# 10,564 products of constants ahead of a decoder step's first conditioning product

## The chip, the cores and the metric

The kernel runs on one core of a Trainium2 chip. The metric is device time in microseconds of one execution; lower is better. A core has a matrix engine (TensorE, PE in the profile, with PEld for its loads of the stationary operand), VectorE (DVE), ScalarE (ACT), GpSimd (POOL) and SyncE (SP, which here only issues DMAs).

## What is computed

One step of a one-layer decoder with D = 2048: T = 288 tokens (256 of a prompt and 8 x 4 samples), all in float32. Cut to what matters here:

```
mod = silu(c) @ w_ada + b_ada                  # 9 conditioning vectors, 2048 x 12288
h = rms(x, g_mix) * (1 + sc_m) + sh_m
proj = h @ w_in                                # 2048 x 9216, then split
ya = b_gate * conv(c_gate * hc)                # short causal convolution
yb = gelu(u) * spatial(rms(gelu(v), g_v))      # 128 x 128 mixing in each chunk
merged = sigmoid(ga) * (ya @ w_pa) + sigmoid(gb) * (yb @ w_pb)
x = x + gt_m * (merged @ w_out)
h2 = rms(x, g_ffn) * (1 + sc_f) + sh_f
gate, up = split(h2 @ w_ffn_in)
x = x + gt_f * ((silu(gate) * up) @ w_ffn_out)
y = rms(x, g_final)
```

## The kernel before

Activations stand transposed, features on the 128 partitions and the 288 tokens along the row. Each weight matrix comes from HBM as blocks of up to 128 x 2048 float32 in tiles tagged `raw`; there are seven such buffers, and a new tile takes the one that comes free first. A block is split by ScalarE and VectorE into a high part `hi` in float32r and a remainder `lo` in float32r (`split`, L448 and L454). A float32 product is made of three float32r products, high by high, high by low and low by high, added in PSUM (`triple`, L224, L227 and L229, or L226 where the order is turned). Nearly all of TensorE's work is this. `ada` products (L388) are the conditioning, plain float32 on 32-column strips of the array.

TensorE's order is the program's order. At the head ScalarE, VectorE and SyncE are put in program order too, up to the point where the early jobs are done; what is recorded ahead of the head is placed by a scheduler. The head is this, in order of TensorE: 24 bf16 products of constant ones into a PSUM tile `idle` that nobody reads (`warm`, L571), the conditioning blocks `a0` with a few more such products between, the first tile of x scaled (`first_tile`), the weights `w0`, the conditioning blocks `a1` (two blocks, the first run after the eighth column tile of `w0`), then `wK`, `wA` and so on:

```
    def warm(n, out=None):
        out = idle if out is None else out
        for _ in range(n):
            PE.matmul(out[:, :T], wb[:, :P], wb, start=True, stop=True)
    ...
    steps = [Do(lambda: warm(24)), a0[0], Do(lambda: warm(5)), a0[1]]
    steps += [Do(first_tile), Do(lambda: warm(6))]
```

SyncE issues the loads in one queue: a0 (two buffers), w0, x's first tile, a1 (two), x's second tile, wK, wA, more of x and wA; in the head each of the seven buffers is taken once before one is taken again. On ScalarE the first compute is `ctt` (half of silu of c), on VectorE the constants `ones`, `mhalf`, `cs`, and then the second half of `ctt` and `cs` (L156, L157).

Of the kernel before, what the change touches and what calls it, by code (L numbers as in the profile page):

```python
# [8 lines left out]
F32 = mybir.dt.float32  # L9
F32R = mybir.dt.float32r  # L10
# [4 lines left out]
P = 128  # L15
D = 2048
T = 288
# [7 lines left out]
RAW = 7  # L25
# [59 lines left out]
def decoder_kernel(tc, d):  # L85
    nc = tc.nc
    from contextlib import ExitStack

    with ExitStack() as es:
        def pool(name, bufs=1, **kw):  # L90
            return es.enter_context(tc.tile_pool(name=name, bufs=bufs, **kw))

        pc = pool("const")
        pw = pool("wstream")
        pslot = pool("slots", SLOTS)
        ptmp = pool("tmp", 5)
        pps = pool("psum", 4, space=bass.MemoryType.PSUM)
        with tc.manual_schedule(engines={nc.tensor.engine}):
            _body(tc, nc, d, pc, pw, pslot, ptmp, pps)


def _body(tc, nc, d, pc, pw, pslot, ptmp, pps):
    ids = [0]

    def nm(s):
        ids[0] += 1
        return f"{s}_{ids[0]}"

    def const(name, shape, dt=F32):
        return pc.tile(shape, dt, tag=name, name=name)  # L110
# [7 lines left out]
    def psmain():  # L118
        return pps.tile([P, 512], F32, tag="main", name=nm("pm"), bufs=4)
# [4 lines left out]
    V, A, G, PE, SY = nc.vector, nc.scalar, nc.gpsimd, nc.tensor, nc.sync  # L124
# [227 lines left out]
    class Step:  # L352
        defer = False
        raw = None
# [209 lines left out]
    wb = const("wb", [P, 288], BF16)  # L564
    G.memset(wb, 1.0)
    idle = psmain()
# [475 lines left out]
        tail.close()  # L1042


    rh1 = h1.__getitem__
    def at(main, plan):
        out, n = [], 0
        for s in main:
            out.append(s)
            if isinstance(s, Blk):  # L1050
                n += 1
                out += plan.pop(n, [])
        assert not plan
        return out
# [101 lines left out]
    for s in steps:  # L1156
# [11 lines left out]
        i = pos[id(s)]  # L1168
# [124 lines left out]
```

## Time and profile before

| | |
|---|---|
| median of 2 runs | 1625.62 us (1625.25 to 1626.0) |
| the profiled execution | 1625.02 us, its span 1623.2 us |
| TensorE busy | 1613.2 us, 99% of the span, 12,645 products |
| VectorE, ScalarE busy | 1015.8 us (63%), 736.2 us (45%) |
| mean granted TensorE clock | 0.998 |
| HBM read | 352.46 MB |

Busy time counts overlapping products once in the engine's total; a group's own busy time adds up the durations of its instructions, which overlap. The digits in the page's strips are tenths of a slice of a fortieth of the span. In a row of the view by windows stand the window, its length, the busy time (and count) of PE, PEld, DVE, ACT and POOL, the granted clock, the DMA share and GB/s. In the timeline stand start, duration, engine (SPq is SyncE's queue), line, operation, and in brackets the idle time ahead and what ended it.

### The profile page before, as it was taken

The page shows a single profiled execution, that of the slowest core. Times are in us where ns is not written, and L with a number is a line of the kernel's source. Part 1 is how long each engine was busy: PE and PEld are TensorE (multiplying, and loading weights), DVE is VectorE, ACT ScalarE, POOL GpSimd, SP SyncE. Part 2 cuts the span into 40 slices and gives each one's busy share as a digit, 9 for nine tenths or more (in the row PEclk, how much of TensorE's full clock was granted, in tenths as well). Part 3 has the DMA queues.
Part 4 walks back from the last instruction along what each step waited for, and adds up shares of the span by engine and source line. Part 5 has one row for each costly group of instructions (what it writes and reads, how often), then busy time and mean ns, then how long its engine had stood idle before and what let it go on. Part 6 is the DMA issues. An engine that isn't in the chain of part 4 may idle for free.

```text
span 1623.2 us, 31599 instructions
## 1 busy us (share of the span) xinstructions
PE 1613.2 (99%) x12645; PEld 1549.3 (95%) x12645; DVE 1015.8 (63%) x2196; ACT 736.2 (45%) x1358; POOL 21.8 (1%) x66
## 2 busy tenths in 40 slices
PE   9999999999999999999999999999999999999997
PEld 8998999999999999999999999999999999999997
DVE  6676788877755567667744555555555555555565
ACT  5533344643444334456633444444444444444454
POOL 0000000000000000011000000000000000000000
PEclk9999999999999999999999999999999999999999
DMA  9887866777877666654576556453464434645341
GB/s 376 324 318 286 313 238 212 273 284 289 298 292 309 261 260 228 241 178 158 185 307 263 207 180 209 156 173 110 164 229 157 168 121 161 225 157 172 110 161 59
DMA packets 59140, 357.60 MB, mean 220 GB/s; under 512 B 6736, under 2 KB 9840, under 8 KB 28272
## 3 DMA queue, kind: packets, MB, share of 16 engines
q1 hardware_dynamic: 58704, 355.45, 60.0%
q8 instruction: 99, 1.62, 0.4%
q14 instruction: 49, 0.40, 0.1%
q10 hardware_dynamic: 288, 0.13, 0.0%
HBM read 352.46 MB, written 3.09 MB: 219 GB/s over the span
## 4 chain that ended last, share of the span: by engine, by line
PE 98%; DMA 1%; DVE 0%; DVEq 0%; ACT 0%; issue 0%; ACTq 0%
PE pm L224 31%; PE pm L227 31%; PE pm L229 30%; PE ada L388 5%; DMA raw<-in_wK 1%; DMA raw<-in_w 0%; DVE st L1023 0%; DMA ct<-in_c 0%; PE px L227 0%; PE px L818 0%; PE px L224 0%; PE px L229 0%; PE px L859 0%; PE px L198 0%; PE px L860 0%; PE px L861 0%
## 5 line engine op out<-in xcount | busy, mean ns | idle before, releaser
L224 PE MATMUL pm<-s,hi 128*128 128x288 f32 (+1 forms) x3750 | 1108.9, 296 | 0.0
L227 PE MATMUL pm<-s,hi 128*128 128x288 f32 (+1 forms) x3750 | 1105.0, 295 | 0.0
L229 PE MATMUL pm<-s,lo 128*128 128x288 f32 (+1 forms) x3738 | 1101.3, 295 | 0.0
L448 ACT CAST hi<-raw 128x512 fp32r<-128x512 f32 (+1 forms) x963 | 587.4, 612 | 812.0 <-PE pm L227 776.7
L454 DVE TENSOR_TENSOR lo<-raw,hi 128x512 fp32r<-128x512 f32 (+1 forms) x849 | 577.2, 681 | 439.2 <-ACT hi L448 426.8
L224 PEld LDWEIGHTS pm<-s,hi 128*128 128x128 f32 x3750 | 705.1, 188 | 15.2 <-issue 13.3
L227 PEld LDWEIGHTS pm<-s,hi 128*128 128x128 f32 x3750 | 704.7, 188 | 0.0
L229 PEld LDWEIGHTS pm<-s,lo 128*128 128x128 f32 x3738 | 702.7, 188 | 0.0
L243 DVE TENSOR_TENSOR lo<-raw,hi 128x512 fp32r<-128x512 f32 x111 | 74.7, 676 | 29.6 <-ACT hi L448 28.9
L388 PE MATMUL ada<-raw,cs 128*32 128x512 f32 (+2 forms) x1152 | 88.3, 452 | 0.0
L388 PEld LDWEIGHTS ada<-raw,cs 128*32 128x32 f32 x1152 | 30.9, 110 | 44.7 <-issue 42.0
L766 DVE TENSOR_TENSOR s<-pm,s 128x288 f32<-128x288 f32 x72 | 32.9, 457 | 19.8 <-PE pm L229 19.8
L298 DVE TENSOR_TENSOR s<-t,s 128x288 fp32r<-128x288 f32 (+1 forms) x76 | 34.6, 459 | 6.4 <-ACT s L296 6.4
L296 ACT CAST s<-t 128x288 fp32r<-128x288 f32 (+1 forms) x76 | 32.5, 433 | 12.9 <-DVE t L798 12.4
L338 DVE SCALAR_TENSOR_TENSOR x<-pm,mod,x 128x256 f32<-128x256 f32 x79 | 37.5, 475 | 0.0
L944 DVE SCALAR_TENSOR_TENSOR t<-t,pm 128x288 f32<-128x288 f32 x42 | 19.1, 454 | 20.6 <-PE pm L229 20.6
L758 DVE TENSOR_TENSOR s<-pm,s 128x288 f32<-128x288 f32 x48 | 21.8, 454 | 10.4 <-PE pm L229 9.5
L337 DVE TENSOR_TENSOR t<-pm,mod 128x32 f32<-128x32 f32 x79 | 15.2, 192 | 18.5 <-PE pm L229 18.5
L743 DVE SCALAR_TENSOR_TENSOR s<-pm,s 128x256 f32<-128x256 f32 x48 | 23.1, 480 | 4.1 <-PE pm L229 4.1
L749 DVE TENSOR_TENSOR s<-s,rb 128x288 f32<-128x288 f32 x48 | 21.5, 449 | 0.0
L172 ACT ACTIVATE t<-x 128x288 f32<-128x288 f32 x29 | 12.9, 445 | 17.4 <-DVE x L341 17.4
L177 DVE TENSOR_TENSOR acc<-acc,t 128x288 f32<-128x288 f32 x33 | 15.0, 456 | 8.2 <-ACT t L172 8.2
(158 smaller groups left out, 479.7 us busy)
## 6 DMA issues: line engine op xcount, KB each, us to landing
raw<-in_fi SPq DMA_DIRECT2D x84, 1024.0 KB, 4.9
raw<-in_a SPq DMA_DIRECT2D x64, 1024.0 KB, 8.8
raw<-in_f SPq DMA_DIRECT2D x64, 704.0 KB, 4.0
raw<-in_wD SPq DMA_DIRECT2D x34, 1024.0 KB, 5.7
raw<-in_aE SPq DMA_DIRECT2D x16, 1024.0 KB, 10.3
raw<-in_wo SPq DMA_DIRECT2D x16, 1024.0 KB, 6.4
raw<-in_wC SPq DMA_DIRECT2D x19, 768.0 KB, 5.7
raw<-in_pa SPq DMA_DIRECT2D x8, 1024.0 KB, 5.9
```

Source lines behind the costliest of these rows:

```text
L224: PE.matmul(out, wh, ah, start=first, stop=False)
L227: end_ = PE.matmul(out, wh, al, start=False, stop=turn and last)
L229: end_ = PE.matmul(out, wl, ah, start=False, stop=last)
L243: lows.pop(0)[1]()
L296: A.copy(hi, a)
L298: V.tensor_tensor(lo, a, hi.bitcast(F32), ALU.subtract)
L338: V.scalar_tensor_tensor(x[:, m, :TP], ps[:, :TP], mod[:, gt0 + m, 0:1], x[:, m, :TP], ALU.mult, ALU.add)
L388: PE.matmul(acc[32 * j : 32 * j + 32, :w], cs[:, kt, :], self.raw[:, o : o + w], start=kt == 0, stop=kt == 15, tile_position=(0, 32 * j), ...
L448: A.copy(hi, self.raw[:, s * 128 : e * 128])
L454: sub()
L743: V.scalar_tensor_tensor(t[:, :TP], ps[:, :TP], t[:, T : T + 1], t[:, :TP], ALU.add, ALU.add)
L766: V.tensor_tensor(a, ps[:, :T], a, ALU.add)
```

## The change

A function `bench` is recorded and called once, behind the definition of the kernel's stages and ahead of everything that the head records (SyncE's loads and TensorE's first 24 products included). It fills one `raw` tile of 128 x 2048 with 0.75, copies it into three more in float32r (one on VectorE, two on ScalarE), and multiplies slices of them. All products write `idle`; no result is read.

```
+    def bench():
+        f = pw.tile([P, 2048], F32, tag="raw", name=nm("bench"), bufs=RAW)
+        V.memset(f, 0.75)
+        rs = []
+        for i in range(3):
+            r = pw.tile([P, 2048], F32R, tag="raw", name=nm("benchr"), bufs=RAW)
+            A.copy(r, f) if i else V.tensor_copy(r, f)
+            rs.append(r)
+        r0, r1, r2 = rs
+
+        def mm(s, m, o=0):
+            PE.matmul(idle[:, o : o + T], s, m, start=True, stop=True)
+
+        def w(k, s=0):
+            return r0[:, P * k + s : P * k + s + P]
+
+        def mv(r, o):
+            return r[:, o : o + T]
+
+        for i in range(48):
+            mm(wb[:, :P], wb)
+        for o in range(64):
+            for i in range(16):
+                mm(w(i % 8), mv(r1, o))
+        for s in range(4, 64, 4):
+            for i in range(12):
+                mm(w(i % 8, s), mv(r1, s))
+        for o in range(0, 64, 8):
+            for i in range(12):
+                mm(w(i % 8), mv(r1, 0), 4 * o // 2)
+        for a in range(0, 64, 4):
+            for b in range(0, 64, 4):
+                for i in range(6):
+                    mm(w(i), mv(r1, a))
+                    mm(w(i), mv(r2, a))
+                    mm(w(8 + i, b), mv(r1, a))
+        for a in range(0, 64, 4):
+            for b in range(0, 64, 4):
+                for i in range(6):
+                    mm(w(i), mv(r1, a))
+                    mm(w(i), mv(r2, b))
+                    mm(w(8 + i), mv(r1, a))
+
+    bench()
```

`P` is 128, `T` 288, `wb` a bf16 tile of ones, `w` a stationary slice and `mv` a moving one.

On TensorE the program of before begins with the 24 products of `warm`; now the 48 of the bench stand ahead of them, then its float32r products (`benchr_99` is r0, `benchr_101` r1, `benchr_103` r2; `pm_96` is `idle`), the first of which waits for VectorE and ScalarE.

```order
L1056 LDWEIGHTS wb
L1056 MATMUL pm_96<-wb 128x288
L1056 MATMUL pm_96<-benchr_101,benchr_99 128x288 [waits DVE_49,Activation_49]
L1056 MATMUL pm_96<-benchr_101,benchr_99 128x288 x1300
```

The three blocks with one moving tile are 1300 products in a row; behind them r1 and r2 take turns to the end of the bench, where `warm` (now L571 behind L1056) follows.

```order
L1056 MATMUL pm_96<-benchr_103,benchr_99 128x288
L1056 MATMUL pm_96<-benchr_101,benchr_99 128x288
L571 LDWEIGHTS wb
```

On ScalarE the two copies stand between `ctt` and the first `hi` of w0:

```order
L155 ACTIVATE ctt<-ct 128x144
L1051 CAST benchr_101<-bench_97 128x2048
L1051 CAST benchr_103<-bench_97 128x2048
L448 CAST hi_10817<-raw_10677 128x512
```

On VectorE the memset and the copy of r0 stand behind `cs`'s own memset and ahead of the second half of `ctt` (L156). On SyncE, before, the queue from a1 on waits only for earlier DMAs (DMAHW names a DMA's semaphore):

```order
L370 DMA raw_111<-in_a 128x1024 [waits DMAHW3_49]
L370 DMA raw_111<-in_a 128x1024 [waits DMAHW4_49]
L370 DMA raw_114<-in_a 128x1024 [waits DMAHW5_49]
L370 DMA raw_114<-in_a 128x1024 [waits DMAHW6_49]
L146 DMA x<-in_x 128x288 [waits DMAHW7_49]
L432 DMA raw_118<-in_wK 128x768 [waits DMAHW0_49]
```

Now the same six rows have waits for the bench's buffers too:

```order
L370 DMA raw_10683<-in_a 128x1024 [waits DMAHW3_49,DVE_49,Activation_49]
L370 DMA raw_10683<-in_a 128x1024 [waits DMAHW4_49]
L370 DMA raw_10686<-in_a 128x1024 [waits DMAHW5_49,PE_49]
L370 DMA raw_10686<-in_a 128x1024 [waits DMAHW6_49]
L146 DMA x<-in_x 128x288 [waits DMAHW7_49]
L432 DMA raw_10690<-in_wK 128x768 [waits DMAHW0_49,PE_49]
```

The first block of a1 takes the buffer of the memset source, free once the copies are made; the second block, and wK behind it, take buffers that TensorE reads to the end of the bench.

## The prediction

> **What bounds the kernel now.** I read the head of the page first, then the chain that ended last.
>
> ```profile
> span 1623.2 us, 31599 instructions
> PE 1613.2 (99%) x12645; PEld 1549.3 (95%) x12645; DVE 1015.8 (63%) x2196; ACT 736.2 (45%) x1358; POOL 21.8 (1%) x66
> ...
> PEclk9999999999999999999999999999999999999999
> ...
> PE 98%; DMA 1%; DVE 0%; DVEq 0%; ACT 0%; issue 0%; ACTq 0%
> PE pm L224 31%; PE pm L227 31%; PE pm L229 30%; PE ada L388 5%; DMA raw<-in_wK 1%; DMA raw<-in_w 0%; DVE st L1023 0%; DMA ct<-in_c 0%; PE px L227 0%; PE px L818 0%; PE px L224 0%; PE px L229 0%; PE px L859 0%; PE px L198 0%; PE px L860 0%; PE px L861 0%
> ```
>
> TensorE is busy for 1613.2 of 1623.2 us at the full granted clock, and the chain is 98% TensorE. Nothing that is put into its queue can hide: one more product moves every later one back by its spacing. So I need the number of added products and the spacing between their starts. A product's own duration is not that spacing, as the grouped view of 890 to 1610 us, a stretch with only the three products of `triple`, shows:
>
> ```profile
> L229 PE MATMUL pm<-s,lo 128*128 128x288 f32 x1816 | 534.9, 295 | 0.0
> L227 PE MATMUL pm<-s,hi 128*128 128x288 f32 x1815 | 534.8, 295 | 0.0
> L224 PE MATMUL pm<-s,hi 128*128 128x288 f32 x1816 | 534.8, 294 | 0.0
> ```
>
> Each lasts 295 ns, yet 5447 of them fit into 720 us: 132.2 ns apiece, since they overlap. The view by windows gives the spacing where engines and DMA are differently loaded:
>
> ```profile
> 220.00:290.00 70.00, 70.00 (x530) 70.00 (x529) 60.39 (x169) 34.86 (x64) 0.00 (x0) 1.00 0.63 219
> 645.00:755.00 110.00, 110.00 (x835) 110.00 (x834) 74.07 (x154) 58.93 (x116) 11.26 (x45) 1.00 0.58 207
> 1300.00:1500.00 200.00, 200.00 (x1516) 200.00 (x1516) 109.94 (x210) 86.72 (x151) 0.00 (x0) 1.00 0.49 164
> 1540.00:1610.00 70.00, 70.00 (x530) 70.00 (x530) 44.81 (x107) 40.44 (x77) 0.00 (x0) 1.00 0.28 95
> ```
>
> The first bracket counts TensorE's products: 70/530 = 132.1 ns, 110/835 = 131.7, 200/1516 = 131.9, 70/530 = 132.1. VectorE's busy share runs from 55% to 86% and the DMA share (the column before GB/s) from 0.28 to 0.63, and the spacing stays. It looks like the price of the product itself, 128x128 by 128x288 in float32r, which is exactly the form that is added.
>
> **The change, part by part.** Counting the loops: 64 x 16 = 1024, 15 x 12 = 180, 8 x 12 = 96, and twice 16 x 16 x 6 x 3 = 4608. That is 10,516 float32r products of 288 columns, behind 48 of bf16. All write one PSUM tile that nobody reads, so no product waits for another engine's eviction.
>
> *The 10,516.* At 132.0 ns, the middle of the windows, they take 1388.1 us. The unknown is the place. The kernel's own spacing varies with the tiles in use, as the starts in the timeline show (two tiles' triples; each from an L224 to the next L224):
>
> ```profile
> 1005.34 0.30 PE L224 MATMUL pm<-s,hi 128*128 128x288 f32 x1
> ...
> 1005.75 0.30 PE L224 MATMUL pm<-s,hi 128*128 128x288 f32 x1
> ...
> 347.71 0.29 PE L224 MATMUL pm<-s,hi 128*128 128x288 f32 x1
> ...
> 348.10 0.29 PE L224 MATMUL pm<-s,hi 128*128 128x288 f32 x1
> ```
>
> Three products take 0.41 us in the first and 0.39 us in the second: 137 and 130 ns apiece. If every added product stood in the worse kind of place, it would be 10,516 x 0.1367 = 1437 us, in the better kind 1367 us. The change walks 256 pairs of places twice, so I take the windows' mean, which is itself a mean over many pairs of tiles.
>
> The added stationary operands are all new loads, as in the kernel: the page counts 12,645 weight loads for 12,645 products, so the windows' spacing already contains them.
>
> *The 48 of bf16, and the slow start.* TensorE's timeline at the head:
>
> ```profile
> 1.12 5.24 PE L571 MATMUL pm<-wb 128*128 128x288 bf16 x24 [1.12 <-POOL wb L565]
> 6.29 1.10 PE L388 MATMUL ada<-raw,cs 128*32 128x64 f32 x64
> ...
> 10.05 1.15 PE L571 MATMUL pm<-wb 128*128 128x288 bf16 x8
> ...
> 1612.72 0.28 PE L571 MATMUL pm<-wb 128*128 128x288 bf16 x1
> ```
>
> The first 24 take 6.29 - 1.12 = 5.17 us. Later, 8 span 1.15 us, of which the last one's own duration is 0.28: 0.87/7 = 0.124 us of spacing. So a start at the full rate would need 24 x 0.124 = 3.0 us, and 2.2 us are a slow start. With the change the 48 pay the slow start and the old 24 behind the bench run at the full rate; the total grows by 48 x 0.124 = 6.0 us, and the slow start is paid once, as before. If the granted clock fell during the bench and the old 24 paid again, it would cost 2.2 us more.
>
> *The constants.* The first product waits for a 2048-element memset and a copy on VectorE, and for a copy on ScalarE. Nearest rows:
>
> ```profile
> 1.07 0.48 DVE L153 MEMSET cs<- 128x512 f32 x1
> ...
> 4.83 0.32 ACT L155 ACTIVATE ctt<-ct 128x144 f32<-128x144 f32 x1 [1.90 <-DMA ct<-in_c]
> ...
> 11.21 0.60 ACT L448 CAST hi<-raw 128x512 fp32r<-128x512 f32 x1
> ...
> 13.19 0.47 DVE L737 COPY s<-pm 128x298 f32<-128x298 f32 x1 [0.17 <-PE pm L509]
> ```
>
> Four times the memset row is 1.9 us, so the source stands at about 3.5 us; VectorE's copy, seven times its 298-column row at most (3.3 us), ends by 6.8 us. ScalarE's copies stand behind `ctt`, which ends at 5.15 us; each takes 4 x 0.60 = 2.4 us, so they end at 7.6 and 10.0 us. The 48 products end at 1.12 + 2.2 + 6.0 = 9.3 us. So the wait is hidden with 1.7 us to spare; without that cover each late microsecond counts once. The third tile, at 10.0 us, is first used after 1300 products. Queued behind these copies are `ctt`'s second half and `cs` on VectorE and the first `hi` on ScalarE, which TensorE only wants after the bench.
>
> *The buffers.* The bench takes four of the seven `raw` buffers. Only the memset source comes free early; three are held to the last product. So on SyncE the load of the second block of a1 now waits for TensorE, and behind it in the same queue stand x's second tile, wK and all of wA.
>
> ```profile
> 6.74 3.01 SPq L370 DMA_DIRECT2D raw<-in_a  x4
> ...
> 10.53 0.33 SPq L432 DMA_DIRECT2D raw<-in_wK  x1
> ...
> 17.87 1.21 PE L388 MATMUL ada<-raw,cs 128*32 128x64 f32 x64
> ...
> 19.79 0.51 ACT L448 CAST hi<-raw 128x384 fp32r<-128x384 f32 x1 [3.90 <-DVE gm L676]
> ...
> 21.01 0.34 PE L226 MATMUL px<-s,lo 128*128 128x298 f32 x1
> 21.69 0.40 PE L227 MATMUL px<-s,hi 128*128 128x298 f32 x1 [0.34 <-DVE s L687]
> ```
>
> From bench end E, the old 24 take 3.0 us, then the order of before follows. The second a1 block is used at 17.87, that is 11.6 us behind the first L388 at 6.29, so at E + 14.6; wK's cast at 19.79 falls at E + 16.5. Before, wK's issue at 10.53 was 9.3 us ahead of its cast. Issued at about E + 2 it has 14.5 us. So nothing starves, with some 5 us of cover; beyond that each microsecond counts once. The early loads (a0, w0, first x, first a1) land long before E. The stall at 21.69 (0.68 us between starts against 0.14) may go with them: I take 0.5 us off, bounded by 0 and 1.
>
> **Sum.** 1388.1 + 6.0 - 0.5 = 1393.6 us. The profiled execution took 1625.02 us, 1.8 us over its span and 0.6 under the median of 1625.62. 1625.0 + 1393.6 = 3018.6; I say 3019.
>
> **The rivals.** *Quiet products run like the warm bf16 ones.* The L571 rows multiply constants, at 0.124 us. If the difference to 0.132 came from real operand values or from neighbours' traffic, 10,516 x 0.124 = 1304 us and the result is 2935. Against it: the spacing doesn't move with DMA share or VectorE's load. For it: no row has float32r on constants. The Trainium skill, page "TensorE: Matmul & The Clock Gate", section "Back-to-back issue gap", gives N/2.4 + 2.5 ns for an isolated warm product whatever the type; that would be 122.5 ns for 288 columns and 2919 us by that rule. The trace agrees for bf16 (0.124) and not for float32r (0.132).
>
> *Places off the kernel's grid cost more.* Of the first block's 64 places only every fourth is a multiple of four elements; 48 x 16 = 768 products start between. Nothing in the trace shows such a start. At worst I price one like a second pass, 132 ns more: 101 us, 3120; at best nothing. The Trainium skill, page "SBUF — State Buffer", section "Specifications (TRN2)", says that SBUF has 16-byte cachelines and that each cross to a new line pays a penalty; by it such a start touches 73 lines rather than 72 if the tile starts on a line, an estimate of 768 x 1.8 ns = 1.4 us. No run here shows it.
>
> *The pairs collide, or suit each other.* In 9216 products two moving tiles are read at equal or regularly shifted places. If all of these cost 137 ns, the sum grows by 9216 x 4.7 = 43 us: 3062. If all cost 130, it falls by 18: 3000.
>
> *Not slower.* Products whose result nobody reads could be dropped when the program is built, or run beside others. To stay within 2% (32.5 us, about what a measurement of this kernel tells from no change) the 10,564 must average under 3.1 ns. Dropped, the time is 1625. The L388 rows speak for some overlap: 64 of them span 1.10 us, some 17 ns each, but they use 32 columns of the array; the new ones use 128, and 17 ns each would still be 180 us. The built program holds all of them.
>
> **How the numbers follow.** The forecast, spacing between 130 and 135 ns (2998 to 3050), 0.74; quiet products 0.06; off-grid places at over a third of the full price (above 3053) 0.08; collisions 0.08, suiting places below 2998 0.035; not slower 0.005. The range: low end 2970, halfway between the forecast and the quiet rival and a little beyond, taking in the suiting places; high end 3087, collisions plus a quarter of the off-grid price (3062 + 25). It leaves out the quiet rival and most of the dear off-grid cases. Slower 0.994, same 0.005, faster 0.001.
>
> **What would show it.** One new TensorE group on `benchr` of 10,516 products, no idle time ahead of it but a fraction of a microsecond at 9 us, and windows inside it with one product per 132 ns, VectorE and ScalarE empty from about 10 us on. The first block's windows (64 places, 16 products each) show whether off-grid places differ. Behind the bench the order of before, its first float32r product 8 us after E. I would be wrong if a window of the bench showed 0.124 or anything above 0.137, or if SyncE's late loads left gaps in the first 20 us behind it.

## The result, and the profile after

The changed kernel takes 3020.61 us (median of two runs, 3020.23 to 3020.99) against 1625.62 us: 1.8581 times as long, 95% interval 1.8501 to 1.8661. The profiled execution took 3020.23 us with a span of 3018.4 us, 1395.2 us more than the span before. The forecast was 3019 us.

The head of the page, the chain that ended last and the two new groups answer to the first rows of before:

```profile
span 3018.4 us, 52735 instructions
...
PE 3008.8 (100%) x23209; PEld 2944.1 (98%) x23209; DVE 1019.5 (34%) x2198; ACT 739.8 (25%) x1360; POOL 21.6 (1%) x66
...
PEclk9999999999999999999999999999999999999999
...
PE 100%; DVE 0%; DVEq 0%; ACT 0%; issue 0%; POOL 0%; POOLq 0%
PE pm L1056 46%; PE pm L224 17%; PE pm L227 16%; PE pm L229 16%; PE ada L388 3%; PE pm L571 0%; DVE st L1023 0%; PE px L227 0%; PE px L224 0%; PE px L818 0%; PE px L229 0%; PE px L859 0%; PE px L198 0%; PE px L860 0%; PE pm L226 0%; PE px L861 0%
...
L1056 PE MATMUL pm<-benchr,benchr 128*128 128x288 f32 x10516 | 1392.6, 295 | 0.0
L1056 PEld LDWEIGHTS pm<-benchr,benchr 128*128 128x128 f32 x10516 | 1392.4, 188 | 0.0
```

All 10,516 products are there (in a product's row float32r operands are printed as f32). A group's busy time, too, counts overlapping products once; the note on the views ahead of the prediction has that wrong. 10,516 times 295 ns would be 3102 us, and the row has 1392.6 us with no idle time in it. That is 132.4 ns apiece, although each lasts 295 ns as before. This row, busy time over count, is read for every experiment below.

The timeline of TensorE at both ends of the bench:

```profile
1.12 7.42 PE L1056 MATMUL pm<-wb 128*128 128x288 bf16 x48 [1.12 <-POOL wb L565]
8.29 3.96 PE L1056 MATMUL pm<-benchr,benchr 128*128 128x288 f32 x28
...
1400.71 3.11 PE L571 MATMUL pm<-wb 128*128 128x288 bf16 x24
1403.76 1.10 PE L388 MATMUL ada<-raw,cs 128*32 128x64 f32 x64
...
1408.88 0.82 PE L501 MATMUL pm<-s,hi 128*128 128x298 f32 x4
```

The bench ends at 1400.71; the first conditioning product stands at 1403.76 instead of 6.29, 1397.5 us later, and the first float32r product at 1408.88 instead of 11.36, again 1397.5 later.

The view by windows, the first three inside the bench (its first block, then the two blocks of pairs), the last in the kernel behind it:

```profile
12.00:140.00 128.00, 128.00 (x963) 128.00 (x963) 0.00 (x0) 0.00 (x0) 0.00 (x0) 1.00 0.02 6
...
182.00:790.00 608.00, 608.00 (x4599) 608.00 (x4598) 0.00 (x0) 0.00 (x0) 0.00 (x0) 1.00 0.00 1
791.00:1400.00 609.00, 609.00 (x4601) 609.00 (x4600) 0.00 (x0) 0.00 (x0) 0.00 (x0) 1.00 0.00 1
1616.00:1686.00 70.00, 70.00 (x534) 70.00 (x533) 60.83 (x169) 35.13 (x65) 0.00 (x0) 1.00 0.62 221
```

128/963 = 132.9 ns, 608/4599 = 132.2, 609/4601 = 132.4, with VectorE and ScalarE empty and the DMAs nearly so. A window counts every product that overlaps it, so two or three of them are neighbours at its edges; over 600 us that is nothing, over 70 us it is half a per cent. The kernel's own spacing was 131.7 to 132.1 ns by such counts, with VectorE, ScalarE and the DMAs at work. By the starts in the trace of before, the same four windows have 132.6, 132.2, 132.1 and 132.5 ns, and the quiet bench lies among them. The last row is the stretch that was 220 to 290 us before: there were 530 products in it then, now 534 (132.6 and 131.5 ns by starts).

### The profile page after: what moved, and what is told of

Same layout as the page of the kernel before. It is cut to its first block, busy times and chain, and to the rows that moved or that the text cites. A ratio compares the mean times of both kernels' runs of the same rounds, so it can differ in the third digit from the quotient of the medians.

```text
span 3018.4 us, 52735 instructions
## 1 busy us (share of the span) xinstructions
PE 3008.8 (100%) x23209; PEld 2944.1 (98%) x23209; DVE 1019.5 (34%) x2198; ACT 739.8 (25%) x1360; POOL 21.6 (1%) x66
## 4 chain that ended last, share of the span: by engine, by line
PE 100%; DVE 0%; DVEq 0%; ACT 0%; issue 0%; POOL 0%; POOLq 0%
PE pm L1056 46%; PE pm L224 17%; PE pm L227 16%; PE pm L229 16%; PE ada L388 3%; PE pm L571 0%; DVE st L1023 0%; PE px L227 0%; PE px L224 0%; PE px L818 0%; PE px L229 0%; PE px L859 0%; PE px L198 0%; PE px L860 0%; PE pm L226 0%; PE px L861 0%
## 5 line engine op out<-in xcount | busy, mean ns | idle before, releaser
L1056 PE MATMUL pm<-benchr,benchr 128*128 128x288 f32 x10516 | 1392.6, 295 | 0.0
L1056 PEld LDWEIGHTS pm<-benchr,benchr 128*128 128x128 f32 x10516 | 1392.4, 188 | 0.0
L677 ACT ACTIVATE s<-x,gm 128x256 fp32r<-128x256 f32 x2 | 1.0, 510 | 1401.4 <-DVE gm L676 1401.4
L766 DVE TENSOR_TENSOR s<-pm,s 128x288 f32<-128x288 f32 x72 | 32.9, 457 | 19.8 <-PE pm L229 19.7
```

The costliest lines, as they stand in the source:

```text
L766: V.tensor_tensor(a, ps[:, :T], a, ALU.add)
L1056: PE.matmul(idle[:, o : o + T], s, m, start=True, stop=True)
```

## The experiments

Apart from the last two, each kernel here was executed once; the two executions of the changed kernel differ by 0.8 us.

**The type.** The bench's three tiles in bf16.

```
-            r = pw.tile([P, 2048], F32R, tag="raw", name=nm("benchr"), bufs=RAW)
+            r = pw.tile([P, 2048], BF16, tag="raw", name=nm("benchr"), bufs=RAW, padded_shape=[P, 4096])
```

> The bench's three tiles are bf16 instead of float32r, everything else as in the changed kernel. Theory (the 132 ns belong to the float32r form): the 10,516 products run at the warm bf16 spacing of 0.123 us, 1293 us instead of 1392, so about 2921 us in all. Rival (the spacing comes from 288 columns and a new stationary load for every product, whatever the type): 132 ns again, 3020 us.

Measured: 2917.01 us. Its groups:

```profile
L1056 PE MATMUL pm<-benchr,benchr 128*128 128x288 bf16 x10516 | 1288.9, 285 | 0.0
L1056 PEld LDWEIGHTS <-benchr 128*128 128x128 bf16 x10516 | 1023.0, 97 | 265.7
```

1288.9/10,516 = 122.6 ns. The same slices and the same number of stationary loads at 9.9 ns less: the surcharge belongs to the type. In the bf16 run TensorE's loader has 265.7 us of idle time, in the float32r run none.

**Two places.** The loops behind the 48 become one, first with the moving slice 7 elements in, then 41.

```
+        for i in range(10516):
+            mm(w(i % 8), mv(r1, 7))       # the second kernel: 41
```

> All 10,516 float32r products at one place of the moving tile, 7 elements in, with 8 stationary slices in turn. In the changed kernel 16 products there stood 130.0 ns apart. Theory (a place has a spacing of its own that lasts): 10,516 x 0.130 = 1367 us instead of 1392, about 2995 us. Rival (the differences between places were passing): 132.4 ns, 3020 us.

> The same with all products 41 elements in, where 16 products stood 136.8 ns apart. Theory (a place has a spacing of its own): 10,516 x 0.1368 = 1439 us, about 3067 us. Rival (passing differences): 132.4 ns, 3020 us.

Measured: 2996.02 and 3054.46 us. Their groups, 7 first:

```profile
L1056 PE MATMUL pm<-benchr,benchr 128*128 128x288 f32 x10516 | 1367.3, 291 | 0.0
```

```profile
L1056 PE MATMUL pm<-benchr,benchr 128*128 128x288 f32 x10516 | 1425.7, 298 | 0.0
```

130.0 and 135.6 ns. A place has a spacing of its own that lasts over 10,516 products; 34 elements further the same work takes 58 us more. The number for 41 was 1.2 ns too high because it came from 14 spacings just behind a change of place: the starts in the trace settle into a pattern that repeats (129, 130, 129, 132 ns at 7; 132, 136, 138, 133, 136, 138, 132, 136, 139 at 41).

**The values.** The source tile is loaded, not filled.

```
-        V.memset(f, 0.75)
+        SY.dma_start(f, d["wA"][0])
```

> The source tile is loaded from a block of w_in instead of filled with 0.75, so the products multiply varied values. Theory (the spacing doesn't depend on values): 132.4 ns again; the load lands some microseconds later than the memset, so 3020 to 3026 us. Rival (constants are cheaper or dearer than data): a bench spacing off by 3 ns or more, 32 us or more either way.

Measured: 3021.37 us.

```profile
L1056 PE MATMUL pm<-benchr,benchr 128*128 128x288 f32 x10516 | 1392.6, 295 | 0.7 <-DVE benchr L1051 0.7
...
L1056 PEld LDWEIGHTS pm<-benchr,benchr 128*128 128x128 f32 x10516 | 1392.4, 188 | 1.0 <-ACT benchr L1051 1.0
```

The same 1392.6 us with a block of weights in place of constants: values play no part here. The operands come late, and the first product waits 0.7 us for them: the cover that the 48 bf16 products give is used up.

**Width.** Every product of the bench reads 512 columns, or 128.

```
-            PE.matmul(idle[:, o : o + T], s, m, start=True, stop=True)
+            PE.matmul(idle, s, m, start=True, stop=True)              # or idle[:, o : o + 128]
-            return r[:, o : o + T]
+            return r[:, o : o + 512]                                  # or o + 128
...
-            mm(wb[:, :P], wb)
+            PE.matmul(idle[:, :T], wb[:, :P], wb, start=True, stop=True)
```

The last two lines keep the 48 bf16 products at 288 columns.

> Every float32r product of the bench reads 512 columns instead of 288 (all of the PSUM tile; the starts stay). float32r stood 132.4 ns apart at 288 columns, bf16 122.5 ns. Theory (the 10 ns are a fixed price of each float32r product): 122.5 x 512/288 + 10 = 228 ns, 2395 us of bench, about 4023 us in all. Rival (the price grows with the columns): 132.4 x 512/288 = 235 ns, 2475 us, about 4104 us.

> Every float32r product of the bench reads 128 columns. Fixed price of 10 ns: 54 + 10 = 64 ns, 677 us of bench, about 2305 us in all. Price by columns: 59 ns, 619 us, about 2247 us. Third theory (the float32r stationary load, 188 ns in the rows against 98 for bf16, has a spacing of its own that shows once the products are short): about 108 ns, the spacing of the kernel's 128-column float32 transposes, 1136 us, about 2764 us.

Measured: 4067.71 and 2803.32 us. Products and loads with 512 columns, then with 128:

```profile
L1056 PE MATMUL pm<-benchr,benchr 128*128 128x512 f32 x10516 | 2439.3, 394 | 0.0
L1056 PEld LDWEIGHTS pm<-benchr,benchr 128*128 128x128 f32 x10516 | 1977.7, 188 | 461.2
```

```profile
L1056 PE MATMUL pm<-benchr,benchr 128*128 128x128 f32 x10516 | 1174.5, 275 | 0.0
L1056 PEld LDWEIGHTS pm<-benchr,benchr 128*128 128x128 f32 x10516 | 1174.4, 192 | 0.0
```

232.0 ns lies between the two theories (228 and 235): the price is neither fixed nor in proportion. 111.7 ns at 128 columns is close to the third theory's number (108) and far from the other two (64 and 59). Narrower products were not tried.

**The same widths in bf16** (both edits above together), to see whether that is the type or the stationary load as such.

> The bench in bf16 with 128 columns for each product. In float32r these stood 111.7 ns apart. Theory (the float32r stationary load holds a short product back, and the bf16 load, 97 ns in the rows against 188, does so less): clearly under 112 ns, by columns alone 122.5 x 128/288 = 54 ns, so 2200 us in all, or up to some 60 ns and 2260 us. Rival (every product with a new stationary operand takes some 110 ns, whatever the type): 2803 us.

> The bench in bf16 with 512 columns. In float32r these stood 232 ns apart, so from 288 to 512 columns each took 0.444 ns. Theory (float32r pays for each column it reads, besides its load): bf16 has a lower slope, 122.5 x 512/288 = 218 ns at most, 2292 us of bench and at most 3917 us in all. Rival (the columns cost alike, and float32r's surcharge is fixed): 232 - 10 = 222 ns, 2335 us of bench and 3960 us.

Measured: 2217.07 and 3899.18 us, by groups (128 columns, then 512, where 211 of the 10,516 product records are missing from the trace):

```profile
L1056 PE MATMUL pm<-benchr,benchr 128*128 128x128 bf16 x10516 | 587.8, 219 | 0.0
```

```profile
L1056 PE MATMUL pm<-benchr,benchr 128*128 128x512 bf16 x10305 | 2259.2, 379 | 11.2
...
L1056 PEld LDWEIGHTS <-benchr 128*128 128x128 bf16 x10516 | 1023.1, 97 | 1246.9
```

55.9 ns at 128 columns and (2259.2 + 11.2)/10,516 = 215.9 at 512. In bf16 each further column costs 0.417 ns from 128 to 288 and again from 288 to 512. float32r's surcharge over bf16 is 55.8 ns at 128 columns, 9.9 at 288 and 16.1 at 512. Both theories hold: the price of the narrow product is the type's, which fits its load of 188 ns against 97. But at 512 the loader sits idle for 461.2 us and float32r still pays more per column (0.444 ns). What that second part is was not tried.

**One stationary slice.**

```
+        for i in range(10516):
+            mm(w(0), mv(r1, 0))
```

> All 10,516 products with one stationary slice at one place, moving place 0, where the changed kernel had 131.8 ns with eight slices in turn. If the stationary place takes part in the spacing, all spacings become alike, at a value between 126 and 139 that is not 131.8: 2957 to 3090 us. If only the moving place matters: 131.8 ns on average, with the same spread between single products, about 3014 us.

Measured: 3013.11 us.

```profile
L1056 PE MATMUL pm<-benchr,benchr 128*128 128x288 f32 x10516 | 1384.9, 294 | 0.0
```

131.7 ns, the 131.8 of eight slices in turn. The second branch holds: by the starts, single spacings repeat as 131, 131, 130, 135 ns, and so they did in the changed kernel at this place, from the fourth on, with eight slices in turn. At this place a change among those slices makes no difference.

**A shift in the kernel itself.** No bench; within each activation slot and each split weight tile the data start four elements further. The tiles grow by that too, so in the built program the slots' data lie 272 bytes further, and those of the eight weight buffers 16 to 240 bytes. All of these are odd multiples of four elements, as the theory asks, but the weights are not shifted alike.

```
-        return pslot.tile(list(shape), dt, tag="s", name=nm("s"), padded_shape=[P, TU])
+        t = pslot.tile([P, shape[1] + 4], dt, tag="s", name=nm("s"), padded_shape=[P, TU + 4])
+        return t[:, 4:]
...
-                hi = pw.tile([P, w], F32R, ..., padded_shape=[P, SEG * 128])
+                hi = pw.tile([P, w + 4], F32R, ..., padded_shape=[P, SEG * 128 + 4])[:, 4:]
```

(`lo` alike.)

> No bench: the kernel before, with all activation slots and all split weight tiles starting 4 elements further. In the bench's second block, where both operands are shifted alike, odd multiples of 4 elements stood 130.2 ns apart and even ones 132.3. Theory (a shift of both by 4 gives that spacing): 11,238 x 2.1 ns = 24 us less, about 1602 us. Rival (over the kernel's many pairs of places it averages out): within 5 us of 1625.

Measured: 1627.20 us against 1625.04 in the same rounds, ratio 1.0013, 95% interval 1.0003 to 1.0022. Two of its windows:

```profile
220.00:290.00 70.00, 70.00 (x532) 70.00 (x531) 60.63 (x169) 34.85 (x64) 0.00 (x0) 1.00 0.63 221
...
1300.00:1500.00 200.00, 200.00 (x1512) 200.00 (x1511) 109.09 (x208) 86.28 (x150) 0.00 (x0) 1.00 0.49 167
```

532 products instead of 530 in one stretch, 1512 instead of 1516 in the other: one stretch gains and the other loses. The rival holds: over the kernel's many pairs it averages out.

**A short bench**, for the gain that the trace shows behind the bench (next section).

```
         for i in range(48):
             mm(wb[:, :P], wb)
-        ...
+        for o in range(0, 64, 8):
+            for i in range(12):
+                mm(w(i % 8), mv(r1, 0), 4 * o // 2)
+        mm(w(0), mv(r2, 0))
```

> The bench keeps its four tiles, the 48 bf16 products and 97 float32r products, and leaves out the other 10,419. Working: the float32r products start at 8.3 to 9.4 us and take 12.8, the old 24 take 3.05, so the first conditioning product stands at 24.2 to 25.2 us instead of 6.29, 17.9 to 18.9 us later. Theory (behind the bench the kernel gains 2.3 us, 0.7 at a stall in the first 25 us and 1.6 because 216 of its products read another slot than before): the total grows by 15.6 to 16.6 us, 1640.6 to 1641.7. Rival (the gain behind the bench came from loads that a long bench lets land early): with E only some 22 us in, the gain is gone and the held buffers cost besides, 1643 us or more.

Measured: 1641.32 us (1640.52 to 1642.01) against 1625.06, ratio 1.0098, interval 1.0081 to 1.0115. TensorE's head:

```profile
1.12 8.24 PE L1056 MATMUL pm<-wb 128*128 128x288 bf16 x48 [1.12 <-POOL wb L565]
9.10 13.03 PE L1056 MATMUL pm<-benchr,benchr 128*128 128x288 f32 x97
21.98 3.12 PE L571 MATMUL pm<-wb 128*128 128x288 bf16 x24
25.02 1.10 PE L388 MATMUL ada<-raw,cs 128*32 128x64 f32 x64
```

The first conditioning product stands 18.7 us later than before. Matching every product's start with the same product's before, the lag is 18.5 us behind the head and 17.0 at the end: a gain of 1.56 us, against 1.58 with the full bench. So the theory holds for the larger part, which needs no long bench.

In the head itself the short bench gains 0.2 us, against 0.7. The rival would put the difference down to the loads, but the trace doesn't show that. At the stall of 21.69 both benches gain alike, 0.38 and 0.36 us. What differs is a pause in the second a1 block, which costs the short bench some 0.5 us:

```profile
36.49 1.09 PE L388 MATMUL ada<-raw,cs 128*32 128x64 f32 x62
37.83 0.30 PE L388 MATMUL ada<-raw,cs 128*32 128x64 f32 x2 [0.25 <-issue]
```

"issue" means that the profile shows nothing that TensorE waited for, and this block's loads had landed by 27.1 us. The cause of the pause stays open; it may belong to this execution alone, the longest of the four.

## Why the prediction was right

**What bounds the kernel** was right: the chain is 100% TensorE, and nothing of the bench hid.

**The 10,516 products** took 1392.4 us from 8.29 to 1400.71, where 1388.1 stood: 132.4 ns instead of 132.0. This term was 4.3 us too small, and most of that comes from the products at the edges of the windows, which were counted in. By starts the four windows have 132.35 ns in the mean, which gives 1391.8 us. The mechanism stands: the spacing taken from windows of the kernel is that of the product itself. It is the same with everything else idle (132.2 to 132.4 in the blocks of pairs) and with other values (the loaded source), and another in bf16.

**The 48 and the slow start** took 8.29 - 1.12 = 7.2 us, where 2.2 + 6.0 = 8.2 stood. The old 24 behind the bench took 3.05, as predicted, so the slow start was paid once. Its length is not constant: in the short bench's execution the same 48 took 8.0.

**The constants** were hidden. Their rows in the timeline after:

```profile
1.93 1.76 DVE L1047 MEMSET bench<- 128x2048 f32 x1 [0.38 <-issue]
3.73 1.23 DVE L1051 CAST benchr<-bench 128x2048 fp32r<-128x2048 f32 x1
...
4.97 3.68 ACT L1051 CAST benchr<-bench 128x2048 fp32r<-128x2048 f32 x2
```

The second tile stands at about 4.97 + 1.84 = 6.8 us, 1.5 us ahead of its use; predicted were 7.6 us and 1.7. The copies were cheaper than bounded (1.23 us against 3.3 on VectorE), and the 48 products that cover them were shorter too.

**The buffers** were right: SyncE waited to the end, and nothing starved. Its waits, then the rows behind the bench:

```profile
SPq L370 <- PE pm L1056: 1391.3, 1, 1391.3
```

```profile
1400.77 0.80 SPq L370 DMA_DIRECT2D raw<-in_a  x2
...
1402.15 0.38 SPq L432 DMA_DIRECT2D raw<-in_wK  x1
...
1413.28 0.56 ACT L448 CAST hi<-raw 128x384 fp32r<-128x384 f32 x1
...
1415.29 1.10 PE L388 MATMUL ada<-raw,cs 128*32 128x64 f32 x64
...
1417.06 0.51 ACT L677 ACTIVATE s<-x,gm 128x256 fp32r<-128x256 f32 x1 [3.23 <-DVE gm L676]
...
1418.20 0.29 PE L226 MATMUL px<-s,lo 128*128 128x298 f32 x1
...
1418.53 0.41 PE L227 MATMUL px<-s,hi 128*128 128x298 f32 x1
```

The second a1 block, issued at 1400.77, is used at 1415.29, 14.6 us behind E as worked out. wK is issued 1.4 us behind E (2 were taken). Its first cast, however, stands at 1413.28, 12.6 us behind E and not 16.5. The prediction took the place of that cast as given. The view of DMAs shows that before, the cast waited for its load: the rows for wK, before and then after, end with the microseconds from issue to landing.

```profile
raw<-in_wK SPq DMA_DIRECT2D x1, 384.0 KB, 9.2
```

```profile
raw<-in_wK SPq DMA_DIRECT2D x1, 384.0 KB, 6.0
```

Before, wK landed at 19.7 us and its cast followed at 19.79. Now it lands at 1408.2, some 5 us ahead of its cast, so the cover was right in size. ScalarE's scaling of the next tile of x (L677) stood right behind that cast, at 20.21; now it follows `gm` at 1417.06, 0.6 us earlier against TensorE's start. The stall at 21.69 shrinks from 0.68 to 0.33 us between starts.

**The gain behind the bench** was mis-sized as well, and lay outside its bounds. I took 0.5 us off with 1 as the bound; the lag falls from 1397.5 us at the first conditioning product to 1395.2 at the end, 2.3 us. 0.7 go in the first 25 us, half of them at that stall. 1.6 go later, in a few stretches, where there is no wait at all: the 534 products instead of 530 are one of them. In the program built with the bench ahead, 216 of `triple`'s products read another slot than before; the stretches lie where these stand, and elsewhere the lag is flat. The conditioning products read other buffers too, but from 290 to 655 us of before, where 384 of them and none of the 216 stand, the lag doesn't move. The short bench reads the same slots as the full one and shows the same 1.6 us. That a place's spacing makes them is fitted by the runs at 7 and 41; those very slots were not measured alone.

The total came out within 1.6 us in part by luck, because terms cancelled: +4.3 for the products, -1.0 for the 48, -1.8 behind the bench, and 0.1 in the old 24.

**The rivals.** *Quiet products like bf16* is out: quiet constants in float32r stand at 132.4 ns. The Trainium skill, page "TensorE: Matmul & The Clock Gate", section "Back-to-back issue gap", gives N/2.4 + 2.5 ns for an isolated warm product, with no word on the type: 55.8, 122.5 and 215.8 for 128, 288 and 512 columns. The runs agree for bf16 (55.9, 122.6, 215.9) and disagree for float32r (111.7, 132.4, 232.0). *Off-grid places* is out as priced: by the starts of the first block, places at a multiple of four elements have 132.8 ns, those 1, 2 and 3 elements past it 135.1, 133.8 and 131.3, together 0.6 ns more than on the grid, 768 x 0.6 = 0.5 us. *Collisions* are out: averaged over the 256 pairs the two blocks have 132.3 and 132.4 ns, single pairs (18 products each) between 129.1 and 135.8. *Dropped products*: all were run.

## What to carry to other kernels

On an engine that is busy all the time the price of an addition is count times spacing between starts, read from starts, or from a window of the kernel where just that form runs and which is long enough that the products at its edges don't count; a row's mean duration (295 ns here) would have given more than double. Spacing depends on the type and the width, so take it from a row of the same form: bf16 at 123 ns would have been 100 us off. And an insertion at the head also changes which buffers later work gets; differences of a microsecond or two, far away and without any wait, may come from that alone.

## What the runs showed of the hardware

A float32r product with a new stationary load is not 288/512 of a wider one: 111.7 ns at 128 columns, 132.4 at 288, 232.0 at 512, where bf16 has 55.9, 122.6 and 215.9. The place of the moving operand decides some 6 ns of it, steadily: 130.0 ns at element 7 and 135.6 at element 41 over 10,516 products each. Why a place is slow stays open. In the blocks of pairs the means over 16 partners run from 131.6 to 133.1 ns with the first place and from 131.9 to 132.9 with the second, and shifting the kernel's slots and weight tiles gained nothing.
